# Last projection part by token halves with GpSimd's sums, softmax scaling on three engines, one bank for filling products

## The chip, the cores and the metric

The kernel runs on one core of a Trainium2 chip. A core has a matrix engine (PE, with PEld for its weight loads), a vector engine (DVE), a scalar engine (ACT), a third elementwise engine (GpSimd, POOL in the profile) and SP, which here only issues DMAs. PE multiplies from SBUF into PSUM, which has eight banks of 128 x 512 f32. The metric is the device time of one execution in microseconds, the median of the runs.

## The reference

A sequence of 512 tokens of width 1024 in f32 goes through two layers of a first kind (three attention branches, merged through projections) and two of a second kind. The change touches the second kind alone:

```python
h = rms_norm(x, norm1) * (1.0 + scale1) + shift1
proj = h @ w_in
...
y_pool = pool_mixer(u, pool_w, pool_scale)
y_nsa = nsa_mixer(q, kv[:, :, 0], kv[:, :, 1], gates, q_norm, k_norm, cmp_pe, cmp_w1, cmp_w2)
mix = jnp.concatenate([y_pool, y_nsa], axis=-1) @ w_out
x = x + gate1 * mix
h2 = rms_norm(x, norm2) * (1.0 + scale2) + shift2
ff = jnp.square(jax.nn.relu(h2 @ w_ff1)) @ w_ff2
return x + gate2 * ff
```

`nsa_mixer` is an attention of eight heads with three branches: compressed keys, selected blocks, and a window. With 512 tokens the last two are full causal softmax attentions of 512 by 512 for each head, scaled by a gate and summed.

## The kernel before

Activations lie transposed in SBUF (features on partitions, 512 tokens along the row). For accuracy each f32 operand is split into a high and a low part, and each product is three matmuls (high x high, low x high, high x low, `products`). Weights come in 364 units of 128 x 1024, in the order of use, each by one DMA on SP's queue into `wraw`. `unit` makes the two parts: ACT casts the high part `wH` (L452), and DVE subtracts it from the raw unit to get the low part `wL` (L453). This subtraction is called a cut below. In the second kind of layer there are three buffers each of `wraw`, `wH` and `wL`.

In a layer of the second kind, `weave` runs four generators side by side at given rates. `main2` makes the projections in: keys, gates, queries, the pool's input and the values. It then makes the projection out in three parts: `o2` (from the pooled features `yp`), the first part of `o2h` (from `yn`, the attention's heads 0 to 3), and the last part of `o2h` (heads 4 to 7). The side chains are `nsa_prep` and `nsa` (the attention), `compressed` and `pool`. After the values, the attention is the long chain, and the products of main2 only fill PE's time between its steps: their PSUM bank is then named `accn` in place of `acc`. The framework's scheduler orders each engine's instructions from these generators; the eight banks are shared by name up to the counts in `CAPS`.

One attention step is one head of one branch, 16 a layer. It makes scores into `S` for four query tiles of 128, 256, 384 and 512 keys (causal). DVE masks them and takes the maximum (L710), ACT makes the exponential and its sum (L711), DVE the reciprocal and the gate (L1759, L1760). Then every tile of p is scaled by its row's factor in SBUF: the first `NACT` = 2 tiles (128 and 256) on GpSimd (L1764), 384 and 512 on DVE (L1766). PE transposes p (L415), ACT casts its high part (L419), DVE subtracts its low part (L420), and PE multiplies with the values into `M`.

`use` (L1507) empties a product's bank: x += gate1 * product, on DVE. For the last part, `use2` does it too and squares the new x on ACT (`stat_step`, L653 for token halves, L660 for all tokens); the squares are summed on DVE (L657 for halves, L661). The first unit of the last part is four products of all 512 tokens (in `main2`); the second is left to `turn` as `emit`, four outputs by token halves (`in_halves`).

`turn` carries the layer into the feed-forward part: the products of half 0, then those of half 1 with the statistics of half 0 in between (`stat_half`: ones products on PE, a power on GpSimd at L578, a broadcast on PE, a copy on ACT at L678), then `h2` for half 0, the statistics of half 1, `h2` for half 1, and the first three units of ff1 by halves. `h2` makes eight tiles of h for each half: two instructions on DVE (L1347, L1349) with one of ACT (L1348) between them.

## Time and profile before

| | us |
|---|---|
| median of three runs | 2391.41 (2388.33 to 2393.7) |
| the profiled execution | 2391.33 |
| its span in the trace | 2389.5 |
| PE busy | 2342.3 (98%) |
| DVE busy | 1640.2 (69%) |
| ACT busy | 1048.7 (44%) |
| GpSimd busy | 264.3 (11%) |

The page's strip of forty slices shows PE at 9 tenths almost all the way. The two layers of the second kind run from about 1200 us on and their middle parts look alike, 593 us apart. In the first of them the values' products end at about 1303, the attention goes on with its filling products to about 1418, the last part of the projection and its statistics to 1441, then comes ff1.

### The profile page before, as it was taken

Reading aid. Unit: us, or ns where it says so; the run is one execution under the profiler, and the core shown is the slowest. Engines: PE = TensorE matmul, PEld = TensorE weight load, DVE = VectorE, ACT = ScalarE, POOL = GpSimd, SP = SyncE. Lnnn points to the kernel's source line nnn. Section 1 sums busy time; section 2 is a strip of 40 time slices with the busy share of each in tenths; the row PEclk is TensorE's granted clock in tenths of the full one; section 3 lists DMA queues with packets and bytes.
Section 4 is the critical chain, followed back from the end, with each engine's and each line's share of the span. In section 5 each row is a group of like instructions: output and inputs, shape, how many; then the busy total and the mean of one; then the engine's idle time right before and its main releaser. Section 6 shows DMA issues by size and latency. Waiting matters only on the chain.

```text
span 2389.5 us, 31476 instructions
## 1 busy us (share of the span) xinstructions
PE 2342.3 (98%) x11684; PEld 1973.3 (83%) x11684; DVE 1640.2 (69%) x3410; ACT 1048.7 (44%) x1930; POOL 264.3 (11%) x254
## 2 busy tenths in 40 slices
PE   8999999999999999999999989999999998999999
PEld 7888888888888888888888778888888876888888
DVE  5679975567588987656579886666647988644342
ACT  6455543434446554343246654332324665433231
POOL 0011010000001001000055310000005531000000
PEclk9999999999999999999999999999999999999999
DMA  5222222245543222225332013555523211223222
GB/s 173 88 80 71 80 80 97 82 156 205 182 159 115 71 80 80 97 88 172 126 102 80 27 37 104 193 194 194 193 97 105 68 35 37 80 94 100 98 93 84
DMA packets 87851, 256.62 MB, mean 107 GB/s; under 512 B 9745, under 2 KB 10769, under 8 KB 87697
## 3 DMA queue, kind: packets, MB, share of 16 engines
q1 hardware_dynamic: 87552, 254.45, 31.9%
q8 instruction: 92, 1.51, 0.3%
q14 instruction: 63, 0.51, 0.1%
q10 hardware_dynamic: 144, 0.15, 0.0%
HBM read 250.37 MB, written 4.19 MB: 107 GB/s over the span
## 4 chain that ended last, share of the span: by engine, by line
PE 93%; DVE 5%; ACT 1%; issue 1%; DMA 0%; POOL 0%; DVEq 0%; ACTq 0%; POOLq 0%
PE acc L406 78%; PE M L406 5%; PE accn L406 4%; PE S L406 3%; PE M L415 3%; DVE p L420 1%; DVE p L710 1%; DVE b L1507 1%; DVE wL L453 1%; ACT p L419 0%; DVE p L1766 0%; ACT p L711 0%; DVE tmp_s L1794 0%; DMA wraw<-wp_in 0%; ACT tmp_s L1792 0%
## 5 line engine op out<-in xcount | busy, mean ns | idle before, releaser
L406 PE MATMUL acc<-h,wH 128*128 128x512 f32 (+2 forms) x2944 | 872.6, 380 | 9.5 <-ACT h L423 7.3
L452 ACT CAST wH<-wraw 128x1024 fp32r<-128x1024 f32 x358 | 375.2, 1051 | 656.8 <-PE acc L406 400.0
L406 PEld LDWEIGHTS acc<-h,wH 128*128 128x128 f32 (+1 forms) x2944 | 537.4, 189 | 106.1 <-ACT h L423 7.3
L453 DVE TENSOR_TENSOR wL<-wraw,wH 128x1024 fp32r<-128x1024 f32 x358 | 437.5, 1223 | 164.9 <-ACT wH L452 156.9
L406 PE MATMUL acc<-h,wL 128*128 128x512 f32 (+1 forms) x1440 | 546.2, 380 | 0.0
L406 PE MATMUL acc<-b,wH 128*128 128x512 f32 (+1 forms) x1696 | 503.9, 374 | 0.0
L406 PEld LDWEIGHTS acc<-b,wH 128*128 128x128 f32 x1696 | 311.8, 189 | 56.3
L406 PEld LDWEIGHTS acc<-h,wL 128*128 128x128 f32 x1440 | 272.7, 190 | 49.6
L406 PE MATMUL acc<-wH,h 128*128 128x512 f32 (+1 forms) x1024 | 310.0, 380 | 0.0
L406 PE MATMUL acc<-b,wL 128*128 128x512 f32 (+1 forms) x784 | 291.5, 372 | 0.0
L406 PEld LDWEIGHTS acc<-wH,h 128*128 128x128 f32 x1024 | 187.2, 188 | 33.7
L406 PE MATMUL acc<-wL,h 128*128 128x512 f32 (+1 forms) x512 | 194.7, 380 | 0.0
L1390 DVE SCALAR_TENSOR_TENSOR b<-acc,keep,b 128x512 f32<-128x512 f32 (+1 forms) x68 | 48.9, 720 | 183.9 <-PE acc L406 183.5
L406 PEld LDWEIGHTS acc<-b,wL 128*128 128x128 f32 x784 | 147.9, 189 | 25.4
L711 ACT ACTIVATE p<-p,nb 128x128 f32<-128x128 f32 x192 | 107.9, 564 | 77.7 <-DVE nb L710 76.7
L1325 DVE SCALAR_TENSOR_TENSOR keep<-keep 128x512 f32<-128x512 f32 x192 | 126.0, 686 | 11.1 <-DMA keep<-w_mod_in 10.9
L578 POOL TENSOR_TENSOR sm_bs<-sm_as,keep 128x4 f32<-128x4 f32 (+1 forms) x48 | 65.7, 1376 | 413.4 <-DVE sm_as L574 374.1
L406 PEld LDWEIGHTS acc<-wL,h 128*128 128x128 f32 x512 | 96.5, 188 | 16.2
L406 PE MATMUL S<-b,b 128*128 128x128 f32 (+3 forms) x480 | 108.9, 338 | 0.1
L710 DVE CUSTOM_DVE_ANT_0 p<-S,keep 128x128 f32<-128x128 f32 x192 | 101.3, 542 | 4.9 <-PE S L406 3.6
L415 PE MATMUL M<-keep,p 128*128 128x128 f32 x608 | 97.4, 275 | 2.7 <-DVE tmp_s L1794 1.0
L406 PE MATMUL M<-p,b 128*128 128x256 f32 (+3 forms) x352 | 81.7, 323 | 10.3 <-DVE p L420 9.0
(294 smaller groups left out, 2898.8 us busy)
## 6 DMA issues: line engine op xcount, KB each, us to landing
wraw<-wp_in SPq DMA_DIRECT2D x364, 512.0 KB, 3.5
keep<-w_mod_in SPq DMA_DIRECT2D x192, 256.0 KB, 3.6
b<-x_in SPq DMA_DIRECT2D x8, 256.0 KB, 6.3
g<-x_in SPq DMA_DIRECT2D x8, 256.0 KB, 4.4
x_spill<-tmp_m SPq DMA_DIRECT2D x8, 256.0 KB, 3.9
g<-x_spill SPq DMA_DIRECT2D x8, 256.0 KB, 3.8
out<-b SPq DMA_DIRECT2D x6, 256.0 KB, 2.0
keep<-parq_in SPq DMA_DIRECT2D x2, 384.0 KB, 6.9
```

Of the source, the lines that this page charges most:

```text
L406: return self.nc.tensor.matmul(out, l, r, start=start, stop=stop)
L415: self.nc.tensor.transpose(out, in_, self.ident[:n, :n])
L420: return self.nc.vector.tensor_sub(l, src, fbits(h))
L452: self.cut_h = nc.scalar.copy(h, raw)
L453: self.cut = nc.vector.tensor_sub(l, raw, fbits(h))
L578: self.pow = nc.gpsimd.tensor_tensor(r[:p, :n], m[:p, :n], self.mhalf[:p, :n], ALU.pow)
L710: nc.vector.tensor_tensor_reduce(p, s, mask, nscale, 3e38, ALU.add, ALU.min, accum_out=nb)
L711: nc.scalar.activation(p, p, AF.Exp, bias=nb, scale=-1.0, accum_out=accum)
L1325: nc.vector.scalar_tensor_tensor(w, w, 1.0, crow[:, T * k:T * k + T], ALU.mult, ALU.mult, accum_out=ms[:, 2 * f + k:2 * f + k + 1])
L1390: nc.vector.scalar_tensor_tensor(x(m)[:, ts], ps[:, ts], mt[:, 40 + m:41 + m], x(m)[:, ts], ALU.mult, ALU.add)
L1507: nc.vector.scalar_tensor_tensor(x(m)[:, ts], ps[:, ts], mt[:, 16 + m:17 + m], x(m)[:, ts], ALU.mult, ALU.add)
```

## The change

In both layers of the second kind:

- **Cuts.** `unit` makes the cut on `self.cutter`: DVE, but GpSimd from the end of the values to the end of the first half of `o2h`. These are ten cuts a layer (four of the pool's input, four of `o2`, two of `o2h`).
- **Scaling of p.** The 256 tile stays on GpSimd, the 128 and 384 tiles go to ACT (a copy with a scale), the 512 tile stays on DVE. `NACT` is gone.
- **One bank.** `accn` may hold one bank instead of two.
- **Last part.** Both units are now left to `turn` and go by token halves, sixteen products of 128 x 256; two outputs share a bank (`shared`). `use2` works on half a tile on DVE each time, the squares are made by halves on ACT, and their sums go to `self.adder`, which is GpSimd from here to the end of `turn` (twelve additions of 128 x 256 a layer, where DVE had three of 128 x 512 and six of 128 x 256).

```diff
@@ -282,6 +282,8 @@
         self.sb = ctx.enter_context(tc.tile_pool(name="sb"))
         self.ps = ctx.enter_context(tc.tile_pool(name="ps", space=bass.MemoryType.PSUM))
         self.units = []
+        self.adder = self.nc.vector
+        self.cutter = self.nc.vector
         self.uid = 0
         self.stream = "m"
         self.acc = "acc"
@@ -450,7 +452,7 @@
             h = self.t((P, 1024), "wH", 4, F32R)
             l = self.t((P, 1024), "wL", 4, F32R)
             self.cut_h = nc.scalar.copy(h, raw)
-            self.cut = nc.vector.tensor_sub(l, raw, fbits(h))
+            self.cut = self.cutter.tensor_tensor(l, raw, fbits(h), ALU.subtract)
         return h, l
 
     def after_unit(self, out, in_):
@@ -475,7 +477,7 @@
             self.products(ps, h, l, k, src.h(k), src.l(k), k == 0, k == KT - 1)
         return ps
 
-    def in_halves(self, jobs, src, use, k0=0):
+    def in_halves(self, jobs, src, use, k0=0, shared=False):
 
 
         made = []
@@ -484,14 +486,20 @@
             ts = slice(256 * half, 256 * half + 256)
             for i, (spec, outs) in enumerate(jobs):
                 if half == 0:
-                    made.append((self.unit(spec), [self.psum("acc") for _ in outs]))
+                    made.append((self.unit(spec), None if shared else [self.psum("acc") for _ in outs]))
                 (h, l), ps = made[i]
                 nk = KT // len(outs)
                 for a, m in enumerate(outs):
+                    if shared:
+                        if m % 2 == 0:
+                            bank = self.psum("acc")
+                        o = bank[:, 256 * (m % 2):256 * (m % 2) + 256]
+                    else:
+                        o = ps[a][:, ts]
                     for k in range(nk):
-                        mm = self.products(ps[a][:, ts], h, l, a * nk + k, src.h(k0 + k, ts), src.l(k0 + k, ts), k == 0, k == nk - 1)
+                        mm = self.products(o, h, l, a * nk + k, src.h(k0 + k, ts), src.l(k0 + k, ts), k == 0, k == nk - 1)
                         if k == nk - 1:
-                            use(m, ps[a], ts)
+                            use(m, o if shared else ps[a], ts)
                         if (a * nk + k) % 4 == 3:
                             yield mm
 
@@ -646,7 +654,9 @@
 
     def stat_step(self, ssq, x, k, ts=None):
         nc = self.nc
-        if k == 0:
+        if k == 0 and ts is not None:
+            nc.scalar.activation(ssq[:, ts], x[:, ts], AF.Square)
+        elif k == 0:
             nc.scalar.activation(ssq, x, AF.Square)
         elif ts is not None:
             sq = self.tmp()[:, ts]
@@ -654,7 +664,7 @@
             if k == KT - 1:
                 self.squares.append(sq)
             else:
-                nc.vector.tensor_tensor(ssq[:, ts], ssq[:, ts], sq, ALU.add)
+                self.adder.tensor_tensor(ssq[:, ts], ssq[:, ts], sq, ALU.add)
         else:
             sq = self.tmp()
             nc.scalar.activation(sq, x, AF.Square)
@@ -1366,6 +1376,7 @@
         self.weave(self.main2(S), [["s", chain(), RATE2], ["c", self.compressed(S), RATEC], ["p", self.pool(S), RATEP]])
         us = [u_s("w_ff1_2", l, P * m) for m in range(NFIRST)]
         hs, first = self.turn(S["emit"], S["ssq"], x, mt[:, 56:64], mt[:, 24:32], us)
+        self.adder = nc.vector
 
         f = {}
         nxt = None
@@ -1497,6 +1508,7 @@
             self.flag("kv")
             self.rate["s"] = RATE3
             self.acc = "accn"
+            self.cutter = nc.gpsimd
 
         parts = {"u": pooled, "k": windows, "g": gates, "q": queries, "w": hidden, "v": values}
         for p in ORDER:
@@ -1515,15 +1527,18 @@
             for i, _ in enumerate(self.quad_unit(("o2h", l, 0, mq), S["yn"], 0, 4 * mq, use)):
                 if i % 2:
                     yield
+        self.cutter = nc.vector
         yield "yn"
         ssq = S["ssq"] = self.new_ssq()
 
-        def use2(m, ps, ts=None):
-            use(m, ps, ts or slice(None))
+        def use2(m, ps, ts):
+
+            nc.vector.scalar_tensor_tensor(x(m)[:, ts], ps, mt[:, 16 + m:17 + m], x(m)[:, ts], ALU.mult, ALU.add)
             self.stat_step(ssq, x(m), m, ts)
 
-        yield from self.quad_unit(("o2h", l, 1, 0), S["yn"], 2, 0, use2)
-        S["emit"] = self.in_halves([(("o2h", l, 1, 1), [4, 5, 6, 7])], S["yn"], use2, 2)
+        self.adder = nc.gpsimd
+        S["emit"] = self.in_halves([(("o2h", l, 1, mq), [4 * mq + i for i in range(4)]) for mq in range(2)],
+                                  S["yn"], use2, 2, True)
 
     def pool(self, S):
         nc, l, par = self.nc, S["l"], S["par"]
@@ -1760,8 +1775,10 @@
                 nc.vector.tensor_tensor(rs, rs, gv[:, :, h, 1 + b], ALU.mult)
                 for i in range(TT):
                     pv = p(P * (i + 1))
-                    if i < NACT:
+                    if i == 1:
                         nc.gpsimd.tensor_scalar(pv, pv, rs[:, i:i + 1], None, ALU.mult)
+                    elif i < 3:
+                        nc.scalar.activation(pv, pv, AF.Copy, scale=rs[:, i:i + 1])
                     else:
                         nc.vector.tensor_scalar(pv, pv, rs[:, i:i + 1], None, ALU.mult)
                 yield
@@ -1885,7 +1902,7 @@
 
 CAPS = {"acc1": 7, "S1": 3, "M1": 5, "b81": 7, "v21": 8, "tmp_m1": 3, "tmp_s1": 5, "tmp_c1": 3, "tmp_t1": 2, "sz1": 3, "cq1": 1,
         "wH1": 4, "wL1": 4, "wraw": 3,
-        "acc2": 7, "accn2": 2, "S2": 3, "M2": 5, "b82": 10, "tmp_m2": 3, "tmp_s2": 5, "tmp_c2": 5, "tmp_p2": 4, "wH2": 3, "wL2": 3}
+        "acc2": 7, "accn2": 1, "S2": 3, "M2": 5, "b82": 10, "tmp_m2": 3, "tmp_s2": 5, "tmp_c2": 5, "tmp_p2": 4, "wH2": 3, "wL2": 3}
 
 
 RATE1 = 1.6
@@ -1902,13 +1919,10 @@
 
 NFIRST = 3
 NLAST = 2
-NLASTP = 2
 
 SLOTS = (1, 3)
 
 GY = 3
-
-NACT = 2
 
 
 NUNITS = 364
```

How the engines' orders change at three places of the first of these layers. A row is the line, the operation, what it writes and reads, and the shape; numbers behind a name tell tiles apart.

PE, the two first filling products of an `o2` unit in the attention stretch, before (`accn_2388` and `accn_2389` are two outputs of the same unit):

```order
L406 MATMUL accn_2388_12139<-b_2198_11424,wH_2386_12135 128x512
L406 MATMUL accn_2388_12139<-b_2197_11423,wL_2387_12136 128x512
L406 MATMUL accn_2388_12139<-b_2197_11423,wH_2386_12135 128x512
L406 MATMUL accn_2388_12139<-b_2198_11424,wH_2386_12135 128x512
L406 MATMUL accn_2388_12139<-b_2197_11423,wL_2387_12136 128x512
L406 MATMUL accn_2389_12153<-b_2197_11423,wH_2386_12135 128x512
L406 MATMUL accn_2389_12153<-b_2198_11424,wH_2386_12135 128x512
L406 MATMUL accn_2389_12153<-b_2197_11423,wL_2387_12136 128x512
```

and now:

```order
L408 MATMUL accn_2388_12139<-b_2198_11424,wH_2386_12135 128x512
L408 MATMUL accn_2388_12139<-b_2197_11423,wL_2387_12136 128x512
L408 MATMUL S_2426_12315<-b_2147_11253,b_2066_10865 128x128 x2
L408 MATMUL S_2432_12331<-b_2147_11253,b_2066_10865 128x256 x2
L417 MATMUL M_2406_12216<-keep_1_61,p_2373_12102 128x128
L408 MATMUL S_2435_12343<-b_2147_11253,b_2066_10865 128x384 x2
L417 MATMUL M_2406_12216<-keep_1_61,p_2374_12103 128x128
L417 MATMUL M_2406_12216<-keep_1_61,p_2373_12102 128x128 x2
L417 MATMUL M_2409_12229<-keep_1_61,p_2374_12103 128x128
L417 MATMUL M_2409_12229<-keep_1_61,p_2373_12102 128x128 x2
L417 MATMUL M_2412_12241<-keep_1_61,p_2373_12102 128x128 x2
L408 MATMUL accn_2389_12153<-b_2197_11423,wH_2386_12135 128x512
```

The second product followed the first at once in another bank; now scores and transposes of the attention stand between, and both have the same bank.

ACT at the end of the attention, before (`wH_2650` and `wH_2654` are the first two units of ff1, `tmp_s_2591` to `b_2267` the attention's last output, `tmp_m` squares):

```order
L1792 COPY tmp_s_2591_12949<-M_2581_12889 64x512
L419 CAST b_2267_11724<-tmp_s_2555_12804 128x512
L650 ACTIVATE keep_1_61<-b_1953_10103 128x512
L660 ACTIVATE tmp_m_2597_12977<-b_1953_10103 128x512
L452 CAST wH_2650_13217<-wraw_13215 128x1024
L660 ACTIVATE tmp_m_2599_12988<-b_1953_10103 128x512
L660 ACTIVATE tmp_m_2601_12999<-b_1953_10103 128x512
L653 ACTIVATE tmp_m_2613_13023<-b_1977_10262 128x256
L452 CAST wH_2654_13248<-wraw_13246 128x1024
L653 ACTIVATE tmp_m_2614_13033<-b_1977_10262 128x256
L653 ACTIVATE tmp_m_2615_13043<-b_1977_10262 128x256
```

and now:

```order
L454 CAST wH_2649_13224<-wraw_13222 128x1024
L1809 COPY tmp_s_2591_12949<-M_2581_12889 64x512
L421 CAST b_2267_11724<-tmp_s_2555_12804 128x512
L658 ACTIVATE keep_1_61<-b_1953_10103 128x256 x2
L663 ACTIVATE tmp_m_2600_12980<-b_1953_10103 128x256
L663 ACTIVATE tmp_m_2602_12991<-b_1953_10103 128x256
L663 ACTIVATE tmp_m_2603_13001<-b_1953_10103 128x256
L663 ACTIVATE tmp_m_2608_13018<-b_1977_10262 128x256
L454 CAST wH_2653_13255<-wraw_13253 128x1024
L663 ACTIVATE tmp_m_2609_13028<-b_1977_10262 128x256
L663 ACTIVATE tmp_m_2611_13039<-b_1977_10262 128x256
L663 ACTIVATE tmp_m_2612_13049<-b_1977_10262 128x256
```

The first ff1 unit's cast (now `wH_2649`) moved ahead of the copy of the attention's last output, and the second's (`wH_2653`) stands ahead of three squares of half 0 (`tmp_m_2609`, `2611`, `2612`).

GpSimd at the turn, before (`sm_bm` is the power of half 0, then of half 1):

```order
L1764 TENSOR_SCALAR p_2537_12736<-p_2537_12736,rsum_2554_12787 128x256
L1764 TENSOR_SCALAR p_2562_12830<-p_2562_12830,rsum_2580_12882 128x128
L1764 TENSOR_SCALAR p_2563_12831<-p_2563_12831,rsum_2580_12882 128x256
L578 TENSOR_TENSOR sm_bm_2623_13100<-sm_am_2622_13099,keep_1_61 128x2
L578 TENSOR_TENSOR sm_bm_2635_13145<-sm_am_2634_13144,keep_1_61 128x2
```

and now:

```order
L667 TENSOR_TENSOR keep_1_61<-keep_1_61,tmp_m_2609_13028 128x256
L667 TENSOR_TENSOR keep_1_61<-keep_1_61,tmp_m_2611_13039 128x256
L667 TENSOR_TENSOR keep_1_61<-keep_1_61,tmp_m_2614_13067 128x256
L667 TENSOR_TENSOR keep_1_61<-keep_1_61,tmp_m_2616_13078 128x256
L586 TENSOR_TENSOR sm_bm_2620_13097<-sm_am_2619_13096,keep_1_61 128x2
L667 TENSOR_TENSOR keep_1_61<-keep_1_61,tmp_m_2617_13088 128x256
L667 TENSOR_TENSOR keep_1_61<-keep_1_61,tmp_m_2622_13108 128x256
L667 TENSOR_TENSOR keep_1_61<-keep_1_61,tmp_m_2623_13118 128x256
L667 TENSOR_TENSOR keep_1_61<-keep_1_61,tmp_m_2625_13129 128x256
L586 TENSOR_TENSOR sm_bm_2638_13183<-sm_am_2637_13182,keep_1_61 128x2
```

Between the softmax scalings and the first power there are now eight additions, the last two of them for half 1, and four more stand ahead of the second power. On DVE the statistics of half 1 (`sm_am_2637`) stand behind the first seven instructions of `h2` for half 0.

## Rows read from the trace of the kernel before

**Rows 1.** Stretches: us, busy us and instructions of each engine, PEclk, DMA, GB/s.
```profile
1255.00:1303.00 48.00, 48.00 (x251) 40.30 (x250) 42.77 (x115) 28.37 (x67) 23.62 (x28) 1.00 0.26 82
1303.00:1345.00 42.00, 37.61 (x212) 30.01 (x211) 39.61 (x113) 30.62 (x83) 20.43 (x26) 1.00 0.08 28
1345.00:1418.00 73.00, 68.52 (x387) 56.77 (x385) 62.76 (x169) 43.30 (x119) 16.37 (x18) 1.00 0.12 40
...
1938.00:2011.00 73.00, 68.61 (x388) 57.19 (x388) 63.45 (x172) 43.71 (x120) 16.36 (x18) 1.00 0.13 43
```

The engines in a row stand in the order PE, PEld, DVE, ACT, POOL.

**Rows 2.** Waits of PE, 1303 to 1418: us in total, times, longest.
```profile
PE M L406 <- DVE p L420: 4.5, 9, 1.0
```

**Rows 3.** DVE's groups, 1303 to 1418: shape, count, busy us, mean ns, idle before.
```profile
L1507 DVE SCALAR_TENSOR_TENSOR b<-accn,keep,b 128x512 f32<-128x512 f32 x16 | 11.8, 744 | 4.3 <-PE accn L406 4.3
...
L453 DVE TENSOR_TENSOR wL<-wraw,wH 128x1024 fp32r<-128x1024 f32 x7 | 8.5, 1218 | 0.0
...
L1766 DVE TENSOR_SCALAR p<-p,rsum 128x384 f32<-128x384 f32 x14 | 6.0, 432 | 0.2
```

**Rows 4.** ACT's groups in the same stretch.
```profile
L711 ACT ACTIVATE p<-p,nb 128x384 f32<-128x384 f32 x14 | 8.6, 617 | 2.8 <-DVE nb L710 2.8
L419 ACT CAST p<-M 128x384 fp32r<-128x384 f32 x16 | 7.7, 482 | 0.0
```

**Rows 5.** GpSimd's groups, 1230 to 1418.
```profile
L1764 POOL TENSOR_SCALAR p<-p,rsum 128x256 f32<-128x256 f32 x16 | 17.2, 1078 | 0.0
L1764 POOL TENSOR_SCALAR p<-p,rsum 128x128 f32<-128x128 f32 x16 | 13.0, 813 | 77.7 <-DVE rsum L1760 56.4 <-ACT tmp_s L1792 5.7 <-ACT p L419 5.1
...
L1546 POOL TENSOR_TENSOR tmp_p<-b 128x511 f32<-128x511 f32 x4 | 4.3, 1081 | 0.0
```

**Rows 6.** Timeline of the turn: start us, us, engine, line, operation, [idle before].
```profile
1419.98 1.12 PE L406 MATMUL accn<-b,wH 128*128 128x512 f32 x2 [2.04 <-ACT b L419]
...
1429.94 0.28 PE L406 MATMUL acc<-b,wL 128*128 128x256 f32 x1
...
1430.14 1.04 ACT L452 CAST wH<-wraw 128x1024 fp32r<-128x1024 f32 x1 [0.57 <-PE acc L406]
...
1431.10 2.25 ACT L653 ACTIVATE tmp_m<-b 128x256 f32<-128x256 f32 x7
...
1434.82 0.58 PE L406 MATMUL M<-keep 128*128 128x1 f32 x2 [4.59 <-DVE keep L657]
...
1437.13 0.72 POOL L578 TENSOR_TENSOR sm_bm<-sm_am,keep 128x2 f32<-128x2 f32 x1 [24.99 <-DVE sm_am L574]
...
1439.57 1.28 DVE L1347 SCALAR_TENSOR_TENSOR tmp_m<-b,keep 128x256 f32<-128x256 f32 x3 [2.62 <-ACT keep L678]
...
1440.71 1.01 PE L406 MATMUL acc<-h,wH 128*128 128x256 f32 x3
```

**Rows 7.** Stretches behind the turn, columns as in rows 1.
```profile
1433.80:1444.00 10.20, 7.87 (x35) 7.71 (x36) 6.63 (x19) 3.10 (x7) 1.58 (x2) 0.50 0.13 47
...
1444.00:1449.00 5.00, 5.00 (x44) 5.00 (x43) 4.82 (x13) 2.85 (x7) 0.00 (x0) 1.00 0.00 0
```

**Rows 8.** Timeline of GpSimd behind the turn into this layer.
```profile
1203.85 9.02 POOL L1600 TENSOR_TENSOR keep<-keep 128x256 f32<-128x256 f32 x1
...
1214.90 0.74 POOL L1605 TENSOR_TENSOR b<-keep 128x256 f32<-128x256 f32 x1
```

**Rows 9.** DVE's groups, 1203.85 to 1212.88.
```profile
L1349 DVE SCALAR_TENSOR_TENSOR h<-tmp_m,keep,h 128x256 fp32r<-128x256 f32 x13 | 6.1, 494 | 0.1
L1347 DVE SCALAR_TENSOR_TENSOR tmp_m<-b,keep 128x256 f32<-128x256 f32 x10 | 4.5, 478 | 0.0
```

**Rows 10.** Timeline of GpSimd, the same pair beside a DVE cut and not.
```profile
1272.69 2.02 POOL L1576 TENSOR_TENSOR tmp_s<-b,b 128x128 f32<-128x128 f32 x2
...
1276.47 0.93 POOL L1576 TENSOR_TENSOR tmp_s<-b,b 128x128 f32<-128x128 f32 x2
```

## The prediction

> **What bounds the kernel now.** I read the page's forty slices first: PE reads 9 nearly everywhere, so a change can only pay where PE idles. Then the table by stage, for the two places of each layer of the second kind that the diff touches. While the values' products are under way PE has no idle time at all [rows 1]. In the attention stretch behind it PE is busy 37.61 of 42 us and 68.52 of 73, so it idles 8.9 us; the second layer's 1938 to 2011 answers to 1345 to 1418 (4.39 us idle beside 4.48) [rows 1]. DVE is the busiest helper there: 39.61 of 42 us, then 62.76 of 73, together 102.4 of 115. ACT has 73.9 of 115 and GpSimd 36.8. The list of waits says whom PE waits for: the low parts of p, which DVE makes, stand at its head with 4.5 us in nine waits [rows 2]. So DVE is late, by about a microsecond at a time, and not ACT.
>
> The other place is the turn into ff1, read from the timeline [rows 6]. PE gets the attention's last output at 1419.98 (after 2.04 us of idling), ends the projection's products at about 1430.2, waits 4.59 us for the sums of squares on DVE (1434.82), gets the power from GpSimd (1437.13), and starts ff1 at 1440.71, with only statistics in between. That is 20.7 us from the first of the last part's products to ff1, of which about 10 are products. Behind the gap the granted clock is 0.50 for 10.2 us [rows 7], of which the last 3.3 lie under ff1.
>
> The profiled run took 2391.33 us, within 0.1 of the median (2391.41), so I sum against 2391.3 without a correction.
>
> **The change part by part.** *Ten cuts a layer go from DVE to GpSimd.* Six of them lie in 1255 to 1303, where PE doesn't idle: I count nothing for these. Four lie in the stretch, each 1.218 us [rows 3]: DVE loses 4.9 us. No cut on GpSimd is in the trace. Its nearest row is L1546, 1.081 us for 511 columns; a cut has 1024, so about 2.2 us, and I take 3.3 for the upper end, with the 1.1 us by which a pair below is held up. Four make 9 to 13 us, and GpSimd loses 14 scalings of 0.813 us (11.4 in all) [rows 5]; it stays at 34 to 38 of 115 us. A cut then takes 1 to 2 us longer from its cast to its end, which the three buffers of weights hide unless PE wants the unit at once.
>
> *The scaling.* Per step DVE gives up 128x384 (0.432 us): 14 in the stretch make 6.0 us [rows 3]. ACT takes 128x384 and 128x128. The trace shows no scaling there; the exponential on 128x384 takes 0.617 us and the cast 0.482 [rows 4], so 14 steps cost between 6.7 us (the wide piece alone, at the cast's price) and 17.3 (both at the exponential's). I take 13, since the narrow piece must be cheaper than the wide one: ACT comes to 87 of 115 us. ACT also makes the exponentials and the casts that open DVE's work, and these queue behind the scaling; that bounds the gain from above. On GpSimd one scaling of 1.078 us is left in place of the pair of 1.89 [rows 5], so p is ready sooner.
>
> Together DVE loses 10.9 of 102.4 us. If PE's idling were all DVE's lateness it would vanish (8.8 us); if the lateness comes from the chain of each softmax step, nothing goes. Only 4.5 of the 8.9 us stand at DVE's p, so I take 4 us a layer, with 0 and 8.8 as ends.
>
> *One bank for the filling products.* Before, the next product's matmuls follow at once in the other bank; now they wait until DVE has emptied the only one (L1507, 0.744 us, 16 in the stretch) [rows 3]. The order puts scores and transposes of the attention in between (fifteen at the place shown), so in the forecast this cover holds and costs nothing. If the cover is gone, each costs up to 0.744 us: a rival below.
>
> *The last part by halves.* The 24 products of 512 columns become 48 of 256, the same columns, so PE's work is unchanged (44 of them in 5.00 us, 0.114 each [rows 7]). What moves is the end of half 0. I count from the time at which the first of these products started before (1419.98). They took 10.2 us, and ACT now casts ff1's first unit ahead of the copy that brings the last output, some 0.7 us later; the last 24 products need 2.7, so PE frees the first unit's weights at 10.2 + 0.7 - 2.7 = 8.2. ACT's next cast waits for that and stands ahead of the last three squares of half 0: 8.2 + 1.04 + 3 x 0.32 = 10.2 [rows 6]. The sums now lie on GpSimd. An addition of 128x256 with two inputs takes 0.74 us there where nothing runs beside it [rows 8]; I use 0.65 to 0.74. But DVE now cuts the second unit of ff1 at 9.4 to 10.6, and GpSimd is held while DVE runs a cut: a pair of small products took 2.02 us, and 0.93 elsewhere [rows 10]. So half 0 is summed at about 11.9 and its statistics are out at 13.0. On GpSimd two additions of half 1 stand ahead of the power, which starts at 13.2 instead of 17.2. By the 2.44 us that before shows from the power to the first h instruction [rows 6], h starts at 15.6: four microseconds earlier.
>
> ff1 doesn't follow at once. On PE the statistics of half 1 stand ahead of its first product, and they need four more additions on GpSimd. Alone these would end near 16.6 and ff1 would start at 17.6, 3.1 us earlier than before. The trace speaks against that: the multiplication L1600, 128x256 on GpSimd, took 9.02 us, though L1605 of the same shape takes 0.74. All that time DVE ran its train of h instructions, 23 of them back to back with two inputs in SBUF each [rows 8, 9]. The same train now starts at 15.6, when two of the four additions are done. DVE's order lets go after seven of its instructions (some 3.0 us, at 0.4 each by the first three [rows 6]), where it waits for the very statistics that lack the additions. So: 18.6, two additions to 20.0 at most, four small products, ff1 at 20.2 to 21. With less of it in the way 17.6, with the power held too about 22. I take 20.2: 0.5 us gained, ends +3.1 and -1.3. The half clock will still end some 3.3 us into ff1.
>
> The Trainium skill (SBUF — State Buffer, section "SBUF: two separate sides") states it as a rule: DVE and GpSimd share a pair of ports, an exclusive lock held for the whole instruction by whichever starts first, against DVE instructions in a two-port mode or with two SBUF inputs. By that rule the 9.02 us row is a lock that was never let go, and it speaks against both moves to GpSimd. Taken literally it gives the second rival's time; without it the turn would be worth 3.1 us a layer and the sum would be 2377.
>
> The sum: 2391.3 - 2 x (4 + 0.5) = 2382.3.
>
> **The rivals.** *All recovered (2368).* DVE was the whole cause (8.8) and GpSimd's additions run freely (3.1): 2391.3 - 2 x 11.9 = 2367.5. For it: the nine waits at p. Against it: ACT's extra 13 us and the 9.02 us row.
>
> *The lock eats it (2392).* A cut on GpSimd holds DVE's scaling and its two-input steps back as DVE's hold GpSimd. Four cuts of 2.2 us hold 8.8 of the 10.9 us that DVE was relieved of; the fifth that is left is worth 0.8 us, and the turn loses 1.3: 2391.3 + 2 x 0.5 = 2392. For it: the blocked pair and the 9.02 us row. Against it: most of DVE's work in the stretch reads PSUM.
>
> *Slower: the single bank (2406).* The fill product's first matmul stands in PE's queue in its place; if DVE's evacuation is late, everything behind it waits, attention too. All 16 exposed cost 11.9 us a layer, less 4.5: 2391.3 + 14.8 = 2406. It decides from seven of the 16 on (6 x 0.744 = 4.5). For it: DVE is still about 80% busy, and evacuations queue behind the softmax. Against it: the attention matmuls that the order keeps between two fills.
>
> *The change doesn't do what it says.* ACT's load turns the waits at DVE's p into waits at ACT's, and nothing moves: 2391. That falls together with the lock's case.
>
> **How the numbers follow.** The forecast (2376 to 2389) 0.48; all recovered 0.12; lock or nothing moved 0.24; single bank 0.16. Two runs of this kernel can be told apart from about 0.2%, 4.8 us: faster is below 2386.6, slower above 2396.2. Faster: 0.42 + 0.12 + 0.02 = 0.56. Slower: 0.13 + 0.01 = 0.14. Same: 0.30. The range leaves out the outer part of the single bank and half of the best case: 2370 to 2396.
>
> **What would show it.** In the stretch DVE's busy time should fall to about 91 us, ACT's rise to 84 to 90, PE's idling fall to about 5. A cut on GpSimd should read about 2.2 us, ACT's scalings 0.3 to 0.6. Waits of accn's matmuls for the evacuation would show the single bank. In the turn, the first power should come some 13 us after the first of the last part's products, GpSimd's last additions of half 1 should read well over 0.7 us or stand idle until DVE's train pauses, and ff1 should start 20 to 21 us on. If ff1 starts at 17 to 18, the additions aren't held and I am wrong there; if PE's idling in the stretch stays near 9, DVE was not what it waited for.

## The result and the profile after

The changed kernel takes 2415.73 us (median of six runs, 2412.1 to 2418.2), the kernel before 2391.85 in the same sessions. The ratio is 1.01 (1.0087 to 1.0113): 24 us slower, where I forecast 9 us faster and a range up to 2396. The profiled execution has a span of 2414.4 us, 24.9 more than before.

Three starts tell where it is lost in the first layer of the second kind. The rows are timelines of the changed kernel (start us, us, engine, line): the first softmax step's widest exponential, the first product of the last part, the first product of ff1.

```profile
1303.67 0.72 ACT L721 ACTIVATE p<-p,nb 128x512 f32<-128x512 f32 x1 [1.33 <-DVE nb L720]
...
1432.75 1.23 PE L408 MATMUL acc<-b,wH 128*128 128x256 f32 x8 [2.02 <-ACT b L421]
...
1451.19 1.20 PE L408 MATMUL acc<-h,wH 128*128 128x256 f32 x4
```

Before, the same three are:

```profile
1293.27 0.73 ACT L711 ACTIVATE p<-p,nb 128x512 f32<-128x512 f32 x1
```

and 1419.98 and 1440.71 [rows 6]. So the attention starts 10.4 us late. The stretch from there to the last part adds 2.4 us more (12.8 late), and the turn gives 2.3 back (10.5 late: 18.4 us from the first product to ff1, 20.7 before). The second layer adds as much and a little more: its first softmax step is 23.6 us late, its ff1 24.0. The loss arises in 1255 to 1303, ahead of the attention stretch, where I had counted nothing. PE had no idle time there [rows 1]; now it has 4.5 us, and 3.4 us at half clock (granted clock 0.51, 1.2 GHz in place of 2.4) lie in it. The next rows are windows of the changed kernel (us, busy us of PE, PEld, DVE, ACT, POOL, PEclk, DMA share, GB/s).

```profile
1255.00:1303.00 48.00, 43.53 (x218) 35.61 (x217) 37.80 (x86) 22.82 (x54) 30.65 (x30) 0.96 0.24 77
...
1265.20:1268.60 3.40, 3.40 (x11) 2.62 (x10) 0.96 (x5) 1.15 (x3) 0.00 (x0) 0.51 0.32 125
...
1345.00:1418.00 73.00, 69.64 (x383) 59.62 (x384) 59.68 (x157) 51.15 (x138) 16.36 (x12) 0.96 0.12 37
```

The last row shows a loss that the starts hide: the attention too has half clock now (1343.7 to 1350.6, right behind three waits of PE for DVE's maxima, 2.3 us together), where before the granted clock was 1.00 [rows 1]. Over the whole execution the trace has 51 us at half clock, 31 before. By these figures the clock accounts for up to 10 of the 24.9 us (an estimate: half of the 20 us more, as if PE had been busy all that time).

What happens in 1255 to 1303 stands in the timelines of GpSimd, DVE and PE:

```profile
1258.73 1.81 POOL L1694 MEMSET b<- 128x2048 f32 x1
1260.49 0.94 POOL L1704 MEMSET b<- 128x1024 f32 x1
1261.40 2.34 POOL L455 TENSOR_TENSOR wL<-wraw,wH 128x1024 fp32r<-128x1024 f32 x1
1269.82 2.39 POOL L455 TENSOR_TENSOR wL<-wraw,wH 128x1024 fp32r<-128x1024 f32 x1 [6.07 <-ACT wH L454]
...
1272.16 1.07 POOL L1591 TENSOR_TENSOR tmp_s<-b,b 128x128 f32<-128x128 f32 x2
...
1259.83 3.96 DVE L1688 CAST tmp_c<-tmp_c 64x64 fp32r<-64x64 f32 x1
...
1278.53 2.59 DVE L1657 TENSOR_TENSOR p<-tmp_s,p 128x256 f32<-128x256 f32 x1
...
1306.03 2.27 DVE L1775 TENSOR_TENSOR rsum<-rsum,keep 128x4 f32<-128x4 f32 x1
...
1264.19 0.30 PE L417 MATMUL M<-keep,tmp_c 64*128 64x64 f32 x2 [2.37 <-DVE tmp_c L1690]
```

GpSimd ran two memsets and the first cut back to back until 1263.74, and DVE's small cast of the compressed keys (64x64) ended only at 1263.79, after 3.96 us. PE stood in front of its result for 2.37 us, and from 1265.2 it ran at half clock for 3.4. Before, the same cast had the memsets alone against it, the copy that PE reads was ready at 1261.70, PE came for it at 1261.76, and GpSimd's first rotation started as soon as ACT's copy was there:

```profile
1259.69 1.65 DVE L1673 CAST tmp_c<-tmp_c 64x64 fp32r<-64x64 f32 x1
...
1261.52 0.18 DVE L1675 COPY tmp_c<-tmp_c 64x64 f32<-64x64 f32 x1
...
1261.76 0.34 PE L415 MATMUL M<-keep,tmp_c 64*128 64x64 f32 x2
...
1267.04 1.12 POOL L1576 TENSOR_TENSOR tmp_s<-b,b 128x128 f32<-128x128 f32 x2 [5.74 <-ACT b L1493]
```

The second effect is in the fence of the changed kernel: GpSimd's second cut waits 6.07 us for ACT's cast, and the first rotation of the queries and keys (L1591) stands behind it, at 1272.16 (before: 1267.04). Of these 5.1 us the second cut makes only 1.1: ACT's copy (L1504) that the rotation reads was itself 4.0 us late, from the first delay. The third are the two small steps on DVE: beside a cut, 128x256 takes 2.59 us (0.41 elsewhere in the same trace) and 128x4 takes 2.27 (0.15 elsewhere). The 15 instructions of DVE that ran over 60 ns longer than the shortest of their form beside a cut, in both layers, lost 25.2 us together by their durations; the cast is not counted among them, since the shortest of its form is itself held.

The critical view, which follows the work that ended last back to what released it, shows that these holds count. Before, the chain is PE's from 1255 to 1303 without a break. In the changed kernel 21 of these 48 us are DVE's, and the chain passes through the cast and the two held steps of 128x256 (start us, us, what):

```profile
1259.83 3.97 DVE tmp_c L1688
...
1278.61 2.51 DVE p L1657
...
1285.68 2.61 DVE p L1657
```

The rest went much as costed. ACT's scalings are 0.609 and 0.403 us, 14.2 for 14 steps where I took 13; a cut on GpSimd takes 2.39 us (2.2).

```profile
L1781 ACT ACTIVATE p<-p,rsum 128x384 f32<-128x384 f32 x15 | 9.1, 609 | 0.0
...
L1781 ACT ACTIVATE p<-p,rsum 128x128 f32<-128x128 f32 x15 | 6.0, 403 | 4.6 <-DVE rsum L1775 4.6
```

### The profile page after: what moved, and what is told of

Its sections match the earlier page's. It is cut to its first block, busy times and chain, and to the rows that moved or that the text cites. A ratio compares the mean times of both kernels' runs of the same rounds, so it can differ in the third digit from the quotient of the medians.

```text
span 2414.4 us, 31602 instructions
## 1 busy us (share of the span) xinstructions
PE 2353.4 (97%) x11732; PEld 1983.6 (82%) x11732; DVE 1632.5 (68%) x3348; ACT 1076.0 (45%) x2002; POOL 301.5 (12%) x266
## 4 chain that ended last, share of the span: by engine, by line
PE 87%; DVE 7%; ACT 2%; POOL 2%; issue 1%; DMA 1%; POOLq 0%; ACTq 0%; DVEq 0%
PE acc L408 74%; PE M L408 5%; PE S L408 3%; PE M L417 3%; PE accn L408 3%; DVE p L422 1%; DMA wraw<-wp_in 1%; DVE p L720 1%; POOL sm_bs L586 1%; ACT p L721 1%; DVE wL L455 1%; ACT wH L454 0%; POOL keep L667 0%; POOL tmp_s L1591 0%; ACT p L421 0%
## 5 line engine op out<-in xcount | busy, mean ns | idle before, releaser
L455 DVE TENSOR_TENSOR wL<-wraw,wH 128x1024 fp32r<-128x1024 f32 x338 | 413.8, 1225 | 169.5 <-ACT wH L454 162.6
L408 PE MATMUL acc<-b,wH 128*128 128x512 f32 (+1 forms) x1760 | 516.0, 371 | 5.9 <-ACT b L421 4.0
L408 PEld LDWEIGHTS acc<-b,wH 128*128 128x128 f32 x1760 | 321.4, 189 | 62.9 <-ACT b L421 4.5
L408 PE MATMUL acc<-b,wL 128*128 128x512 f32 (+1 forms) x816 | 301.3, 370 | 0.0
L408 PEld LDWEIGHTS acc<-b,wL 128*128 128x128 f32 x816 | 154.9, 190 | 25.2
L408 PEld LDWEIGHTS S<-b,b 128*128 128x128 f32 x480 | 79.2, 189 | 17.5 <-DVE nb L720 8.1
```

Of the source, the lines that this page charges most:

```text
L408: return self.nc.tensor.matmul(out, l, r, start=start, stop=stop)
L455: self.cut = self.cutter.tensor_tensor(l, raw, fbits(h), ALU.subtract)
```

## The experiments

Times are medians; "before" in each session lies between 2390.6 and 2391.9. A run's profile shows the same starts as above; where I give the delay of the first softmax step, it is against 1293.3.

**Which part.** Cuts alone (the kernel before with `self.cutter = nc.gpsimd` as in the change); all cuts back, or those of the pool's input alone; the scaling alone (the change's lines in `step`, with all else as before).

```diff
 cuts_back:    after values():      -self.cutter = nc.gpsimd   +self.cutter = nc.vector
 u_cuts_back:  moved to where o2 begins (self.cutter = nc.gpsimd ahead of yield "yp")
```

> The kernel before, with the ten cuts a layer on GpSimd and nothing else of the change. Theory Q (GpSimd's queue: a cut waits there for ACT's cast and for the weight buffer, and the steps that prepare the attention stand behind it): the first softmax step of each layer starts 8 to 10 us later, PE idles there, 2408 to 2412 us. Rival S (ACT's scaling or the single bank costs the time, the cuts are hidden as I counted them): 2386 to 2393 us.

> The changed kernel with all cuts on DVE again. Theory Q: the 8 to 10 us a layer come back, 2395 to 2400 us. Rival S: 2411 to 2418 us, as the changed kernel.

> The changed kernel with the four cuts of the pool's input on DVE again, those of o2 and of the first half of o2h still on GpSimd. Theory Q: only cuts that stand ahead of the first softmax steps do harm; those of the pool's input are most of these, so 2397 to 2404 us. If the cuts of o2 in the attention stretch do the harm (GpSimd's port held against DVE): 2409 to 2416 us.

> The kernel before, with the scaling of p shared by three engines and nothing else of the change. Theory Q: within 5 us of the kernel before (2387 to 2395 us), with DVE's busy time in the attention stretch down by 6 us. Rival S: ACT is late for the next step's exponentials, 2398 to 2410 us.

Measured: cuts alone 2422.41 (1.0129, 1.0113 to 1.0146), cuts back 2395.8 (1.0018, 1.0009 to 1.0028), pool's cuts back 2396.24 (1.0022), scaling alone 2394.29 (1.0006, 0.9997 to 1.0016). The first softmax step is 11.6 us late with the cuts alone, 1.1 early with all cuts back, and 0.3 late with the four back. So in the changed kernel the cuts are the loss, and the four of the pool's input nearly all of it: 19.5 of the 19.9 us that come back with all ten. The cuts alone cost 31.6 us, 10 more than the upper end of what I had expected: beside the late start, the attention takes 3.3 and 3.6 us longer in the two layers. The scaling costs or gains nothing that can be told.

**One bank, the last part.** The kernel before with one bank alone; with the last part and one bank; with the halves alone and the sums on DVE.

```diff
 bank_alone:       -"accn2": 2   +"accn2": 1
 halves_dve_sums:  the change's in_halves and use2, self.adder = nc.vector throughout
```

> The kernel before with one bank for the filling products and nothing else of the change. If the attention's matmuls cover the evacuation: 2388 to 2395 us. If all evacuations are exposed (0.744 us, 16 a layer): up to 2415; seven of them: 2401.

> The kernel before with the last part by halves, its sums on GpSimd, and one bank (two banks and this last part together need more PSUM than there is); cuts and scaling as before. The turn of the changed kernel took 18.4 us from the last part's first product to ff1, 2.3 less than before: 2391 minus 4.6 gives 2386, plus what the one bank costs.

> The kernel before with the last part by halves and its sums on DVE, two banks, cuts and scaling as before. If the halves bring the turn's gain: 2385 to 2388 us, like the run with GpSimd's sums without the bank's cost. If GpSimd's sums bring it: 2390 to 2394 us.

Measured: 2395.28 (1.001, 0.9998 to 1.0021), 2402.42 (1.0053, 1.0037 to 1.007), 2392.47 (1.0005, 0.9996 to 1.0014). My slower rival, the single bank at 2406, isn't seen in the run with one bank alone. The 11 us that the last part lost with one bank, where I had expected a gain, don't lie in the turn but in the attention stretch (131 us from its first widest exponential to the copy of its last output on ACT, 125 before), whose order had changed. One bank alone had not lost them. What the second expectation says of PSUM is wrong: the last part by halves fits beside two banks, as the run with DVE's sums and two more below have it. The halves with DVE's sums missed too: the turn was 1.5 and 2.3 us shorter in the two layers, but the second layer's attention, in another order, took 2.1 us longer, and the total didn't move. That made me ask what an order alone is worth.

**The order alone.** `RATE3 = 9.0` in place of 10.0: the same instructions, interleaved otherwise.

> The kernel before with the attention's generator advanced 9 steps for each filling product in place of 10: the same instructions, in another order in the attention stretch. It tells how far an order alone moves the time, against which the runs with one part alone are to be read. If orders matter little: within 3 us of before. If as much as the run with the second cut alone suggests, which lost 8 us in the attention: 5 to 20 us a run.

Measured: 2402.28 (1.0051, 1.0034 to 1.0068), 10.5 us lost by order alone. The trace has 44 us at half clock, 31 before, so up to 7 us of it are the clock (half of the difference, an estimate). A part tried alone moves the scheduler's order too, so single totals here can carry some 10 us that are not the part's own. What follows rests on two pairs of runs that keep every order (this next one against before, and the one with the first cut back against the changed kernel), and on where in the trace the time is lost.

**One instruction, every order kept.** The first cut of the pool's input alone on GpSimd. No engine's order changes otherwise.

```diff
+self.cutter = nc.gpsimd if g == 0 else nc.vector    # in pooled()
```

> The kernel before with one cut a layer on GpSimd, that of the first unit of the pool's input; every engine's order is otherwise that of before, row for row. In the changed kernel a copy on DVE (the compressed keys' cast) took 3.96 us there, until GpSimd's cut ended, PE waited 2.37 us for it, and 3.4 us at half clock followed. If GpSimd's cut holds DVE's copy by the shared port: 2.4 + 1.7, 4 us a layer, 2397 to 2401 us, and the copy takes about 4 us. If the port is no matter: 2389 to 2393 us.

Measured: 2397.98 (1.0029, 1.0018 to 1.004), 6.2 us, 3.1 a layer. Timelines of DVE, GpSimd and ACT, and PE's waits from 1255 to 1303 (us in total, times, longest):

```profile
1259.02 3.97 DVE L1689 CAST tmp_c<-tmp_c 64x64 fp32r<-64x64 f32 x1
...
1260.60 2.34 POOL L455 TENSOR_TENSOR wL<-wraw,wH 128x1024 fp32r<-128x1024 f32 x1
...
1296.45 0.73 ACT L721 ACTIVATE p<-p,nb 128x512 f32<-128x512 f32 x1
```

```profile
PE M L417 <- DVE tmp_c L1691: 2.4, 1, 2.4
```

The cast ends at 1262.99, 0.05 us after GpSimd's cut; PE waits 2.4 us where it waited for nothing; the first softmax step is 3.2 us late, about the 3.1 a layer of the medians (in this execution, one of the longer of the seven, ff1 is 4.2 late, behind another 3.4 us at half clock at 1340). The Trainium skill (SBUF — State Buffer, section "SBUF: two separate sides") has it as an exclusive lock on a shared pair of ports, which goes to whichever engine starts first. The cast's end right behind the cut agrees, in this direction too: GpSimd holds DVE. Who starts first is less plain: the cast stood from 1259.02, and a memset (1259.68) and the cut (1260.60) that began after it went ahead.

**The others.** The second cut alone; the third and fourth; the six of o2 and o2h; the changed kernel with only the first back; and with dummies in place of the four cuts, which wait for the raw unit and not for ACT's cast.

```diff
 u2_alone:   g == 1      u34_alone: g >= 2      first_back: g > 0 (in the changed kernel)
 u_dummies: +nc.gpsimd.tensor_tensor(junk, raw, raw, ALU.subtract)
```

> The kernel before with one cut a layer on GpSimd: that of the second unit of the pool's input, ahead of the attention's preparation in GpSimd's order (in the changed kernel GpSimd idled 6.07 us ahead of it, until ACT's cast). If the wait does the harm: 4 to 5 us a layer, 2399 to 2402 us. If only GpSimd's 2.4 us count: 2394 to 2397 us.

> The kernel before with two cuts a layer on GpSimd: those of the third and fourth unit of the pool's input, which stand between the preparation's steps. If GpSimd's own time counts there: 2.4 to 5 us a layer, 2396 to 2402 us. If only the wait ahead of the second unit's cut did harm: 2390 to 2394 us.

> The kernel before with the six cuts of o2 and of the first half of o2h on GpSimd, none of the pool's input. GpSimd scales two tiles of p here (one in the changed kernel), behind the cuts in its queue. In the run with all ten cuts alone the attention step at 1351 was 5 us later than the one before it: if that is these cuts' doing, 2398 to 2402 us; if not, 2390 to 2394 us.

> The changed kernel with the first cut of the pool's input on DVE again, the other nine still on GpSimd. If the first cut's hold of DVE starts the delay: 4 us a layer come back, 2405 to 2410 us, and the first softmax step starts 4 us sooner than in the changed kernel (1303.7). If the nine others do all of the harm: 2413 to 2418 us.

> The changed kernel with all cuts on DVE, and on GpSimd in their place, for the four units of the pool's input of each layer, a subtraction of the same size that reads the raw unit alone, so that it waits for the unit's DMA and not for ACT's cast (its result is not used). The base is the run with all cuts back, 2395.8 us. If the harm is the waiting of GpSimd's queue for the cast: 2396 to 2402 us. If it is the 9.4 us of GpSimd's time themselves, ahead of the attention's preparation: 2408 to 2414 us.

Measured: 2410.53, 2406.89, 2408.84, 2407.22 and 2409.42. With the first cut back every order is that of the changed kernel, but for the cut itself; 8.5 us of the total come back, 4.2 a layer, as expected of the port, and the attention of the first layer starts 7.0 us sooner, where I had expected 4. The third and fourth delay the first step by 6.3 us. With the second cut alone the first softmax step is only 1.4 us late, and the rest of its loss came later, in the order of the last attention steps. At the first softmax step the three runs of single cuts thus add up to 3.2 + 1.4 + 6.3 = 10.9 us, against 11.6 for all ten cuts alone and 10.4 in the changed kernel.

The six cuts of o2 and o2h alone lost 17.8 us, more than either of my expectations, though the first step came 1.5 us early: the first layer's attention took 134.6 us, 124.7 before. DVE's steps held by these cuts make only 1.8 us of that; the rest is open (GpSimd's two scalings behind the cuts, or the order). In the changed kernel the same six cost nothing (2396.24 with them, 2395.8 without). So it holds for the changed kernel, and not for the kernel before, that only the pool's cuts do harm.

The dummies came out as expected of GpSimd's time itself (the first step is 5.5 us later than with the cuts back), but they don't tell time from waiting cleanly: two of the four ran ahead of the memsets (1251.35 and 1255.51), where no cut of the change ran, and GpSimd idled 5.42 us for the raw unit's DMA in place of 6.07 for ACT's cast. One of them held the same cast of DVE (3.50 us), and PE waited 4.2 us for its result. So the wait for ACT's cast isn't needed for the harm.

**A shorter hold.** Each cut on GpSimd as four of 128x256, all else as in the change.

```diff
-self.cut = self.cutter.tensor_tensor(l, raw, fbits(h), ALU.subtract)
+for i in range(n):    # n = 4 on GpSimd, cs the i-th quarter of the columns
+    self.cut = self.cutter.tensor_tensor(l[:, cs], raw[:, cs], fbits(h[:, cs]), ALU.subtract)
```

> The changed kernel with each cut on GpSimd as four instructions of 128x256. If a held instruction of DVE gets its turn between two instructions of GpSimd: DVE's holds shrink from 2.1 to 2.8 us to about 0.7, and 5 to 8 us a layer come back, 2400 to 2406 us. If GpSimd's train holds the port as DVE's train did in the 9.02 us row: nothing comes back, 2414 to 2422 us.

Measured: 2409.24 (1.0074, 1.0059 to 1.0089), 6.5 us back, half of what I expected of the port. GpSimd's and DVE's timelines:

```profile
1261.85 2.78 POOL L458 TENSOR_TENSOR wL<-wraw,wH 128x256 fp32r<-128x256 f32 x4
...
1260.28 4.39 DVE L1691 CAST tmp_c<-tmp_c 64x64 fp32r<-64x64 f32 x1
...
1279.45 0.76 DVE L1660 TENSOR_TENSOR p<-tmp_s,p 128x256 f32<-128x256 f32 x1
```

The two halves of the answer stand side by side. DVE's two-input step, 2.59 us beside a whole cut, takes 0.76 beside pieces: it gets its turn between two of them. The cast of the compressed keys doesn't: it waits for all four (4.39 us). That isn't a matter of casts as such: casts of 128x256 got in between two pieces in the same trace (0.82 us at 1289.09, 0.49 at 1280.46). The first softmax step stays as late as in the changed kernel (1303.4), though the two held steps of the chain are gone (0.76 and 0.41), so another path was about as late. What comes back in the first layer lies in the attention.

**DVE's load.** One more instruction of 128x512 on DVE in each softmax step, its result unused.

```diff
+if i == TT - 1:
+    nc.vector.tensor_scalar(self.t((P, T), "junk", 1), pv, 1.0, None, ALU.mult)
```

> The kernel before with one more instruction of 128x512 on DVE in each of the 16 softmax steps a layer (it copies the scaled tile, and nobody reads the copy). If PE's idling in the attention stretch is DVE's load, as my prediction took it: 0.5 to 0.6 us a step, 8 to 10 us a layer, 2407 to 2411 us. If it is the chain of each step, DVE has the time: 2391 to 2396 us.

Measured: 2404.37 (1.0058), 6.7 us a layer, between the two; the order moved with it, so it doesn't tell load and chain apart. Taking 5 us of load away (the scaling alone: PE idles 8.0 us from the first step to the last copy, 8.8 before) gave back 0.8.

**Without cuts and with two banks.** What is left of the change, with the sums on GpSimd and on DVE.

```diff
-"accn2": 1            +"accn2": 2
-self.cutter = nc.gpsimd   (both)
-self.adder = nc.gpsimd   +self.adder = nc.vector   (scale_halves_dve)
```

> The changed kernel with all cuts on DVE and two banks for the filling products: scaling on three engines and the last part by halves with GpSimd's sums. With the cuts back and one bank it took 2395.8 us. If the one bank was what kept the turn's gain (1 to 2 us a layer) from the total: 2386 to 2390 us, faster than before. If the order of the attention decides, as the run at rate 9 suggests: anywhere from 2388 to 2400 us.

> As the run beside it, with the squares' sums on DVE in place of GpSimd. If GpSimd's sums are worth their moving: 1 to 3 us slower than that. If DVE's sums do as well, since the stretch behind the products has DVE free: the same within 2 us.

Measured: 2389.61 (0.9994, 0.9984 to 1.0004) and 2388.23 (0.9987, 0.9978 to 0.9995). The second is ahead of both kernels, by some 3 us of 2391 (1 to 5 by the interval): scaling on three engines and halves, with the sums on DVE. As its order differs from before, the 3 us can't be put down to these parts. GpSimd's sums aren't worth moving: the 1.4 us between the two are too few to be told apart, but the turns point the same way (20.0 and 20.1 us in the two layers with GpSimd's sums, 19.3 and 17.9 with DVE's).

The first of the two differs from the run with the cuts back (2395.8) in the one bank alone, and is 6.2 us shorter (0.9984 to 1.0004 against 1.0009 to 1.0028). So beside the new scaling and the last part the single bank, with the order that comes with it, costs some 3 us a layer: the first layer's attention takes 127.2 us with one bank and 124.3 with two.

## Why the prediction was wrong

The forecast was 2382.3 and the result 2415.73, 33 us more. The cuts make 20 of these (they come back with all ten on DVE). The other 13 are what the kernel without them (2395.8) still lies over the forecast: the relief of 8 us didn't come, and the single bank costs about 6 (an estimate from the runs above).

- **The cuts in 1255 to 1303: wrong, and the step that failed.** "Six of them lie in 1255 to 1303, where PE doesn't idle: I count nothing for these." That PE is never idle says that everything arrives in time, not by how much. What the compressed keys' cast leads to was ready at 1261.70, and PE came for it at 1261.76; 2.4 us of delay had no cover. I asked what PE waits for and didn't follow what is queued on GpSimd in that stretch (memsets, rotations, powers, copies of p: 23.6 of 48 us busy [rows 1]), most of it ahead of the attention's first step. In place of nothing the four cuts of the pool's input cost 19.5 us, and the attention of the first layer started 10.4 us late.
- **The lock: the right mechanism, in the wrong place and of the wrong size.** I had it from the 9.02 us row [rows 8, 9] as DVE holding GpSimd, used it in the turn, and priced it in the attention stretch at 8.8 of the 10.9 us relieved, so that the rival ended at 2392. It is worst where a short DVE step in a chain meets a long GpSimd instruction: 2.27 us instead of 0.15 for 128x4.
- **The relief of DVE in the stretch: too large.** I took 4 us a layer; scaling alone with its 5 us less of DVE's time changed nothing that can be told. So the waits at DVE's p [rows 2] weren't DVE's load alone; how much of them is each step's chain, no run shows.
- **The single bank: right by itself, wrong beside the rest.** Alone it is covered (2395.28, not told from 2391.6 at this size). In the first layer of the changed kernel PE's filling products waited twice for the bank, 2.1 us in all, and without the cuts the second bank is worth 6.2 us, where the forecast had nothing.
- **The turn: right in direction, 0.5 forecast, 2.3 measured in the first layer and 1.6 in the second.** Turns without the new last part lie between 18.9 and 21.4 us in these runs, turns with it between 17.8 and 20.1. The power of half 0 came 12.2 us after the first product (1444.91; I said 13.2), h started 15.6 us after it (as I said), ff1 18.4 (I said 20.2). GpSimd's additions took 0.64 us each, one 1.45 beside a DVE cut and the last 0.70, so the train hardly held them: two of the last four were through when it began at 1448.30, as I had said, but the other two went ahead of the train and held its first two instructions instead (1.39 us together, 0.87 for another pair):

```profile
1441.29 3.48 POOL L667 TENSOR_TENSOR keep<-keep,tmp_m 128x256 f32<-128x256 f32 x4 [0.58 <-ACT tmp_m L663]
1444.91 1.67 POOL L586 TENSOR_TENSOR sm_bm<-sm_am,keep 128x2 f32<-128x2 f32 x1
1446.56 2.85 POOL L667 TENSOR_TENSOR keep<-keep,tmp_m 128x256 f32<-128x256 f32 x4
...
1448.30 1.39 DVE L1357 SCALAR_TENSOR_TENSOR tmp_m<-b,keep 128x256 f32<-128x256 f32 x2 [2.30 <-ACT keep L688]
```

  The power, 1.67 us instead of 0.72, ran beside a DVE cut (1444.78, 1.22 us). Of the 2.3 us the clock took some back: the stretch at half clock is 10.2 us as before, but 5.1 of them now lie under ff1, and 3.3 did.
- **What stays open:** how the 10.4 us divide between the hold of DVE, GpSimd's queue and the new order. With every order kept the first cut is worth 3.1 us a layer alone and 4.2 when it is taken back out of the ten; the others were only measured in kernels whose order differed. The chain passes through held DVE steps, but shortening two of them didn't bring the attention forward. Why the cuts alone cost 32 us and the whole change 24 isn't settled either; the three-engine scaling has one tile less in GpSimd's queue behind the cuts, which would fit.

## What to carry to other kernels

A stretch in which the bottleneck engine never idles isn't a stretch where work can be moved for nothing: look at each short step that feeds it, and at how early it arrives. Work moved from DVE to GpSimd is charged three times, by its own longer time, by GpSimd's queue behind it, and by DVE's steps that stand still while it runs; the longest waits here stood beside the longest instructions, and cutting these up gave 6.5 of 24 us back, so above all keep them away from chains. Where a scheduler makes the order, measure what an order alone is worth (here 10 us) before reading single parts by their totals, and read the granted clock of each stretch beside them: PE's wait of 2.37 us here was followed by 3.4 us at half clock.

## What the runs showed of the hardware that I had not expected

- DVE's small steps can stand for nearly the whole of a GpSimd instruction: 128x4 took 2.27 us and 128x256 2.59 beside a cut of 2.39, and 0.15 and 0.41 elsewhere.
- Against a train on GpSimd DVE's instructions fare differently: the cast of 64x64 waited for the end of four pieces (4.39 us in the first layer, 4.38 in the second), while two-input steps (0.76 us) and casts of 128x256 (0.49 and 0.82) got in between two pieces. What decides it, no run shows.
- Beside memsets alone the cast of 64x64 ends 0.05 us behind the last of them too (1.65 us before, in both layers; five casts of 32x128 right behind it take 1.14 together).
- Moving a cut between engines moved the time at half clock as well: 51 us in the changed kernel, 31 before, 41 with the first cut back.
